# The two FFNs of a hybrid decoder layer: half of the tokens at a time, seven block products in place of eight

## The chip, the cores and the metric

The kernel runs on one core of a Trainium2 chip. The metric is the device time of one launch in microseconds (us), the median over several runs. The engines are named as the profile names them: PE is TensorE (PEld its weight loads), DVE is VectorE, ACT is ScalarE, POOL is GpSimd, SP is SyncE, which here only issues DMAs.

## The reference

One layer over 1032 tokens (1024 of a prompt, 8 of a decoding batch), all in float32. What the change touches are the two SwiGLU blocks, `ffn1` and `ffn2`, each with D_MODEL = 1024 and D_FF = 2816:

```python
def rmsnorm(x, g):
    y = xf * lax.rsqrt(jnp.mean(xf * xf, axis=-1, keepdims=True) + EPS)
    return y * g

def swiglu_half(x, g, w_gate, w_up, w_down):
    u = rmsnorm(x, g)
    return x + 0.5 * ((jax.nn.silu(u @ w_gate) * (u @ w_up)) @ w_down)

def hybrid_layer(...):
    h = swiglu_half(x, ffn1_norm, ffn1_w_gate, ffn1_w_up, ffn1_w_down)
    u = rmsnorm(h, mix_norm); z = u @ w_in          # latent attention, retention, gates
    ...
    h = h + merged @ w_out
    h = swiglu_half(h, ffn2_norm, ffn2_w_gate, ffn2_w_up, ffn2_w_down)
    gate = sigmoid(rmsnorm(h, ple_norm) @ w_ple_gate)
    h = h + gate * (p_emb @ w_ple_proj)             # then a last rmsnorm
```

## The kernel before

**Layout.** Activations stand transposed: features on the 128 partitions (8 tiles `h[0..7]` of 128 features), tokens along the free axis. The 1032 tokens are worked in three chunks of 344 (`CHUNKS`).

**Products.** A float32 product is made of three passes of split numbers: `split` (L92 to L94) casts a tile to a rounded high part on ACT (L93) and takes the rest, source minus high part, on DVE (L94); `mm3` (L127 to L130) then issues high x high, high x low, low x high, each a matmul with its own weight load, summed in PSUM. Weights come from DRAM by `Ring.load` (L103) in blocks of 128 x 1024 and are split once each.

**The norm.** `norm_steps` (L183) multiplies h by the gain, splits it into the two halves of `u` (ACT L199, DVE L200), squares it (ACT L144, L148) and adds the squares on POOL (L149). `rstd` (L162) sums over partitions with small matmuls (L169), iterates on DVE (`newton`, L133 to L137) and spreads the result back with matmuls (L177). The factor r itself is multiplied into the gate and up products after PSUM (L235, L238).

**An FFN** (`ffn`, L221) goes over the 22 tiles of D_FF in groups of three (the last of four). For each tile f it loads a gate and an up block, and for each chunk makes both products over 8 tiles of features (48 matmuls of 344 columns), then silu and the multiplication, and splits the result into `mid`. After a group come its down products into PSUM, over the group's tiles, added to h in SBUF (L274). One FFN so has 22 x 3 x 48 + 22 x 8 x 3 x 3 = 4752 matmuls of 344 columns. Nothing but the weights is moved: h and u stay in SBUF.

**At the seams** the work is interleaved by hand: the last group's down products hand each finished tile of h to the next norm (`nxt`, called step by step between products), the start of the first FFN splits u tile by tile while products run, and the last chunk group of `wout` does the same for the second FFN's norm (L980 and following). `pend`, `tick` and `flush` hold back the steps that wait for other engines. Behind the first FFN stand the value products of retention (`value_tile`, L321 to L323: 24 matmuls of 256 columns for each tile of 128 tokens), which need u alone; in front of the second FFN stands `wout`, behind it the per-layer embedding (`ple_gate`, L1034 and following).

The order on each engine is made from the program by a scheduler, within what the tiles' buffers allow; each engine runs its own list in that order.

## Time and profile before

| | |
|---|---|
| time, three runs | 2558.05, 2555.63, 2557.17 us; median 2557.17 us |
| span of the profiled execution | 2553.2 us, from its first to its last instruction, 4.0 us under the median of the runs |
| PE busy | 2519.5 us (99%), 16,612 matmuls |
| PEld busy | 2433.6 us (95%) |
| DVE busy | 1251.2 us (49%) |
| ACT busy | 655.8 us (26%) |
| POOL busy | 209.6 us (8%) |
| HBM traffic | 147.47 MB read, 19.94 MB written, 66 GB/s over the span |

A row of the timeline gives the start in us from the span's begin, the duration, engine, source line, operation, output and inputs, shape, count, and in brackets how long the engine had been idle and what ended that. A row of the windows view gives a stretch, then the busy time and count of instructions of PE, PEld, DVE, ACT and POOL, the granted TensorE clock, the share of the DMA engines and GB/s. A row of a line's instructions gives min/median/max in ns and the first and last start. Matmul durations overlap, since they are pipelined: the step from start to start is what one costs.

### The profile page before, as it was taken

Reading aid. Unit: us, or ns where it says so; the run is one execution under the profiler, and the core shown is the slowest. Engines: PE = TensorE matmul, PEld = TensorE weight load, DVE = VectorE, ACT = ScalarE, POOL = GpSimd, SP = SyncE. Lnnn points to the kernel's source line nnn. Section 1 sums busy time; section 2 is a strip of 40 time slices with the busy share of each in tenths; the row PEclk is TensorE's granted clock in tenths of the full one; section 3 lists DMA queues with packets and bytes.
Section 4 is the critical chain, followed back from the end, with each engine's and each line's share of the span. In section 5 each row is a group of like instructions: output and inputs, shape, how many; then the busy total and the mean of one; then the engine's idle time right before and its main releaser. Section 6 shows DMA issues by size and latency. Waiting matters only on the chain.

```text
span 2553.2 us, 40552 instructions
## 1 busy us (share of the span) xinstructions
PE 2519.5 (99%) x16612; PEld 2433.6 (95%) x16612; DVE 1251.2 (49%) x2744; ACT 655.8 (26%) x1302; POOL 209.6 (8%) x247
## 2 busy tenths in 40 slices
PE   8999999999999999999999999999999999999998
PEld 7999999999999999999996669999999999999997
DVE  6434334434354666522467776844434343343645
ACT  5121121211233111211145652431211211212521
POOL 3000000000022001100042100200000000000211
PEclk9999999999999999999999999999999999999999
DMA  4111111110113121221124436111111110111111
GB/s 151 42 59 51 41 59 42 50 42 34 58 71 117 62 77 58 98 77 64 54 78 129 121 107 217 51 58 42 50 42 44 53 53 34 58 42 50 40 36 67
DMA packets 82507, 171.08 MB, mean 67 GB/s; under 512 B 9401, under 2 KB 51586, under 8 KB 82322
## 3 DMA queue, kind: packets, MB, share of 16 engines
q1 hardware_dynamic: 76098, 150.67, 17.6%
q0 software_dynamic: 6224, 17.82, 2.0%
q8 instruction: 130, 2.13, 0.3%
q14 instruction: 55, 0.45, 0.1%
HBM read 147.47 MB, written 19.94 MB: 66 GB/s over the span
## 4 chain that ended last, share of the span: by engine, by line
PE 94%; DVE 3%; DMA 1%; ACT 1%; issue 1%; POOL 0%; SPq 0%; POOLq 0%; DVEq 0%; ACTq 0%
PE ps L128 27%; PE ps L129 27%; PE ps L130 27%; PE ps L732 2%; PE ps L768 1%; PE ps L757 1%; PE ps L177 1%; PE ps L323 1%; PE ps L321 1%; PE ps L322 1%; DVE u L200 1%; PE ps L169 1%; DMA raw<-in_wout_dram 0%; PE ps L906 0%; PE ps L880 0%
## 5 line engine op out<-in xcount | busy, mean ns | idle before, releaser
L128 PE MATMUL ps<-u,w 128*128 128x344 f32 (+2 forms) x3072 | 990.6, 323 | 7.6 <-ACT w L93 7.6
L129 PE MATMUL ps<-u,w 128*128 128x344 f32 (+2 forms) x3072 | 987.0, 321 | 3.5 <-DVE u L200 3.5
L130 PE MATMUL ps<-u,w 128*128 128x344 f32 (+2 forms) x3072 | 982.8, 320 | 0.1
L128 PEld LDWEIGHTS ps<-u,w 128*128 128x128 f32 x3072 | 578.4, 188 | 9.6 <-ACT w L93 7.6
L129 PEld LDWEIGHTS ps<-u,w 128*128 128x128 f32 x3072 | 577.2, 188 | 6.4 <-DVE u L200 5.5
L130 PEld LDWEIGHTS ps<-u,w 128*128 128x128 f32 x3072 | 577.9, 188 | 1.1 <-DVE w L94 0.5
L93 ACT CAST w<-raw 128x1024 fp32r<-128x1024 f32 (+1 forms) x198 | 203.4, 1042 | 776.7 <-PE ps L130 757.0
L130 PE MATMUL ps<-mid,w 128*128 128x344 f32 x1248 | 399.7, 320 | 0.1
L129 PE MATMUL ps<-mid,w 128*128 128x344 f32 x1248 | 399.7, 320 | 0.0
L128 PE MATMUL ps<-mid,w 128*128 128x344 f32 x1248 | 399.6, 320 | 0.0
L274 DVE SCALAR_TENSOR_TENSOR h<-ps,h 128x344 f32<-128x344 f32 x336 | 172.0, 515 | 242.0 <-PE ps L130 239.8
L94 DVE TENSOR_TENSOR w<-raw,w 128x1024 fp32r<-128x1024 f32 (+1 forms) x198 | 239.1, 1219 | 63.5 <-ACT w L93 63.0
L130 PEld LDWEIGHTS ps<-mid,w 128*128 128x128 f32 x1248 | 235.4, 189 | 0.4 <-DVE w L94 0.4
L128 PEld LDWEIGHTS ps<-mid,w 128*128 128x128 f32 x1248 | 235.2, 188 | 0.0
L129 PEld LDWEIGHTS ps<-mid,w 128*128 128x128 f32 x1248 | 235.0, 188 | 0.0
L238 DVE TENSOR_TENSOR m<-ps,r 128x344 f32<-128x344 f32 x132 | 68.1, 516 | 336.4 <-PE ps L130 336.4
L149 POOL TENSOR_TENSOR acc<-acc,sq 128x344 f32<-128x344 f32 x83 | 84.1, 1013 | 1677.9 <-ACT sq L148 1676.6
L93 ACT CAST mid<-m 128x344 fp32r<-128x344 f32 x156 | 74.9, 480 | 353.3 <-DVE m L239 316.6
L235 DVE TENSOR_TENSOR sg<-ps,r 128x344 f32<-128x344 f32 x132 | 68.0, 515 | 167.5 <-PE ps L130 166.0
L236 ACT ACTIVATE sg<-sg 128x344 f32<-128x344 f32 x132 | 64.6, 489 | 227.8 <-DVE sg L235 227.8
L94 DVE TENSOR_TENSOR mid<-m,mid 128x344 fp32r<-128x344 f32 x156 | 80.9, 519 | 48.0 <-ACT mid L93 46.9
L200 DVE SCALAR_TENSOR_TENSOR u<-h,gains,u 128x344 fp32r<-128x344 f32 x96 | 65.1, 686 | 30.7 <-ACT u L199 30.6
(247 smaller groups left out, 2321.4 us busy)
## 6 DMA issues: line engine op xcount, KB each, us to landing
ct<-in_cache_dram SPq DMA_DIRECT2D x128, 128.0 KB, 2.1
raw<-in_f1gate_dram SPq DMA_DIRECT2D x22, 512.0 KB, 3.5
raw<-in_f1up_dram SPq DMA_DIRECT2D x22, 512.0 KB, 3.5
raw<-in_f1down_dram SPq DMA_DIRECT2D x22, 512.0 KB, 4.5
raw<-in_f2gate_dram SPq DMA_DIRECT2D x22, 512.0 KB, 3.5
raw<-in_f2up_dram SPq DMA_DIRECT2D x22, 512.0 KB, 3.5
raw<-in_f2down_dram SPq DMA_DIRECT2D x22, 512.0 KB, 4.8
hs_d<-h POOLq DMA_DIRECT2D x3, 1376.0 KB, 6.1
```

The source lines that it names most:

```text
L93: act.copy(dst_hi, src)
L94: dve.tensor_tensor(dst_lo, src, dst_hi.bitcast(F32), op=ALU.subtract)
L128: pe.matmul(ps, w[:, 0, ws], x[:, 0, xs], start=start, stop=False)
L129: pe.matmul(ps, w[:, 0, ws], x[:, 1, xs], start=False, stop=False)
L130: pe.matmul(ps, w[:, 1, ws], x[:, 0, xs], start=False, stop=stop)
L149: pool.tensor_tensor(acc, acc, sq[:, :n], op=ALU.add)
L200: dve.scalar_tensor_tensor(u[k][:, 1, xs], h[k][:, xs], gain(gi, k), u[k][:, 0, xs].bitcast(F32), op0=ALU.mult, op1=ALU.subtract)
L235: dve.tensor_tensor(s[:, :n], pg[:, :n], r[:, xs], op=ALU.mult)
L236: act.activation(s[:, :n], s[:, :n], AF.Silu)
L238: dve.tensor_tensor(m[:, :n], pu[:, :n], r[:, xs], op=ALU.mult)
L274: dve.scalar_tensor_tensor(hv, ps[:, :n], 0.5, hv, op0=ALU.mult, op1=ALU.add)
L732: pe.matmul(ps[:, :w], qc[hd][:, i * P:(i + 1) * P], kc[hd][:, j:j + w], start=True, stop=not diag)
```

## The change

Both FFNs are rewritten; the rest of the layer is moved only where it joined onto them.

**Halves and blocks.** A half of the tokens (`tp`, 516 tokens) is worked at a time, as two column blocks of 258 (`HC`). Every product is cut into 2 x 2 blocks (features by halves, outputs by two tiles, tokens by the two column blocks) and made of seven block products (`ORDER`) of sums and differences, which are collected in PSUM and, for three of them, in copies: `unit` makes the two sets of seven for a pair of outputs, gate and up (`pair`) or two pairs of output tiles (`down`). A pair unit has 168 matmuls of 258 columns, a down unit 42 for each pair of D_FF tiles in its group. `GROUPS` has 3, 3, 2, 2 and 1 pairs. One FFN so has 5544 matmuls of 258 columns.

**Weights.** `Stream` loads eight raw blocks for a unit (2 outputs x 4 blocks, 128 x 512 for gate and up), makes four sums or differences of each four blocks on POOL (L267, L269, L287, L292) and splits fourteen blocks (ACT L102, DVE L103), five ahead of the product. This is done again for the second half of the tokens.

**Gated values.** The products of gate and up come out as four blocks. They are added, silu and multiplication made, three more sums made (L406 to L421, POOL), and seven blocks split into `mid`, which stays in SBUF.

**Inputs.** The seven block sums of the normed input (`b`) for the first half are made at the start from h (`first`); those of the second half are made during the first half's products (`second`), written to DRAM (L570), and read back in one go (L607) when the first half's last pair unit is done. r is now multiplied in before the products.

**Seams.** h goes to DRAM after each FFN (L477) and is read from there (L584, L632); the norms that were interleaved with products stand by themselves.

The core of the diff; of the two `evac`, the first is a pair unit's and the second a down unit's:

```diff
+HC = T // 4
+GROUPS = [(0, 1, 2), (3, 4, 5), (6, 7), (8, 9), (10,)]
...
+    ORDER = (0, 1, 2, 3, 4, 6, 5)
...
+        def early(self, r):
+            for s in range(2):
+                n = r["a11", s].shape[-1]
+                r["s1", s] = self.rawp.tile([P, 512], F32, tag="q", name="ws")[:, :n]
+                pool.tensor_tensor(r["s1", s], r["a21", s], r["a22", s], op=ALU.add)
+            for s in range(2):
+                pool.tensor_tensor(r["a21", s], r["a11", s], r["a21", s], op=ALU.subtract)
...
+        def make(self, units):
+            r = self.load(units[0])
+            self.early(r)
+            for i in range(len(units)):
+                nxt = None
+                for q, part in zip(ORDER, ("a11", "s1", "a11", "a12", "a21", "a12", "a22")):
+                    for s in range(2):
+                        yield self.split(r[part, s])
+                    if q == 0:
+                        for s in range(2):
+                            pool.tensor_tensor(r["a11", s], r["s1", s], r["a11", s], op=ALU.subtract)
+                    elif q == 2 and i + 1 < len(units):
+                        nxt = self.load(units[i + 1])
+                    elif q == 3:
+                        for s in range(2):
+                            pool.tensor_tensor(r["a12", s], r["a12", s], r["a11", s], op=ALU.subtract)
+                    elif q == 4 and nxt:
+                        self.early(nxt)
+                r = nxt
...
+    def unit(stream, b, kh, evac, tick, ahead=None):
+        x, y, z = ([take(), take()] for take in (xbank, ybank, zbank))
+        for q in ORDER:
+            if ahead is not None:
+                next(ahead, None)
+            for s in range(2):
+                w = stream.take()
+                ps = (x, z, x, y, x, x, z)[q][s][:, :HC]
+                for j in range(kh):
+                    js = slice(j * P, (j + 1) * P)
+                    t = b(q, j)
+                    pe.matmul(ps, w[:, 0, js], t[:, 0], start=q in (0, 1, 3) and j == 0, stop=False,
+                              skip_group_check=True)
+                    pe.matmul(ps, w[:, 0, js], t[:, 1], start=False, stop=False, skip_group_check=True)
+                    pe.matmul(ps, w[:, 1, js], t[:, 0], start=False, stop=j == kh - 1, skip_group_check=True)
+                evac(q, s, ps)
+                tick(at)
...
+            def evac(q, s, ps):
+                if q < 3:
+                    t = kept[s, q] = et()
+                    act.copy(t, ps)
+                    return
+                if q == 5:
+                    t = et()
+                    if s == 0:
+                        act.activation(t, ps, AF.Silu)
+                    else:
+                        dve.tensor_tensor(t, ps, gated[q], op=ALU.mult)
+                else:
+                    t = kept[s, {3: 0, 4: 1, 6: 2}[q]]
+                    dve.tensor_tensor(t, t, ps, op=ALU.add)
+                    if s == 0:
+                        defer(1, act.activation, t, t, AF.Silu)
+                    else:
+                        eng = dve if q == 6 else pool
+                        defer(2, eng.tensor_tensor, t, t, gated[q], op=ALU.mult)
...
+                def evac(q, s, ps):
+                    if q in (0, 2):
+                        t = et()
+                        act.activation(t, ps, AF.Copy, scale=0.5)
+                        defer(1, pool.tensor_tensor, hv, hv, t, op=ALU.add)
+                    else:
+                        dve.scalar_tensor_tensor(hv, ps, 0.5, hv, op0=ALU.mult, op1=ALU.add)
+                    if last and q == 5:
+                        sp.dma_start(dst[:, k - 1:k + 1, both(tp)], ht[:, k - 1:k + 1])
...
+                    if tp == 0 and seen == NF // 2:
+                        while side[0] is not None:
+                            tick(99)
+                        bt = new_b()
+                        for q in ORDER:
+                            sp.dma_start(bt[:, :, q].bitcast(F32), b_d[:, :, q])
...
+    ffn("f1", 0, a["xT"], hs_d, b1_d)
...
+        read_h(ht, hs_d)
+        wv0 = [ring.load("rv", i) for i in range(2)]
+        for c in range(NCH):
+            for _ in norm_steps(tmp, h, c, 1, u, r):
+                pass
...
-        u, r, wv0 = ffn(ring, tmp, mp, "f1", h, u, r, up, ws, lambda c: norm_steps(tmp, h, c, 0, u, r, c == 0),
-                        lambda: [ring.load("rv", i) for i in range(2)], to_mix)
...
+            wout(g, c, wo)
+            c0, n = CHUNKS[c]
+            sp.dma_start(h2_d[:, :, c0:c0 + n], ht[:, :, c0:c0 + n])
...
+    ffn("f2", 2, h2_d, h3_d, b2_d)
...
+    read_h(ht, h3_d)
```

**How the order moves: POOL in the FFN.** Before, the whole stretch of the first FFN on POOL holds the additions of squares for the norms at its two ends (`acc`, `sq`) and the writes of h for later; between them nothing:

```order
L149 ISA
L149 TENSOR_TENSOR acc<-acc,sq 128x344 x26
L331 DMA hs_d<-h 1024x1x344
L149 TENSOR_TENSOR acc<-acc,sq 128x344 x7
L331 DMA hs_d<-h 1024x1x344
```

Now one pair unit in the middle of an FFN half has these (`wq` a raw weight block, `ws` a sum, `e` a block of gated values):

```order
L380 TENSOR_TENSOR e<-e 128x258
L287 TENSOR_TENSOR wq<-ws,wq 128x512
L380 TENSOR_TENSOR e<-e 128x258
L287 TENSOR_TENSOR wq<-ws,wq 128x512
L406 TENSOR_TENSOR e<-e 128x258
L411 TENSOR_TENSOR e<-e 128x258
L416 TENSOR_TENSOR e<-e 128x258
L292 TENSOR_TENSOR wq<-wq 128x512
L267 TENSOR_TENSOR ws<-wq 128x384
L269 TENSOR_TENSOR wq<-wq 128x384
L421 TENSOR_TENSOR e<-e 128x258
```

POOL had no instruction between the two norms; it now has fourteen for each pair unit (a second L292, L267 and L269 follow), each with two inputs in SBUF.

**DVE in the FFN.** Before, one D_FF tile and one chunk on DVE (`sg`, `m` the gate and up values, `mid` the split result, `w` the split weights, two blocks for three chunks):

```order
L235 TENSOR_TENSOR sg<-ps_1453,r 128x344
L94 TENSOR_TENSOR w<-raw,w 128x1024
L238 TENSOR_TENSOR m<-ps_1454,r 128x344
L239 TENSOR_TENSOR m<-m,sg 128x344
L94 TENSOR_TENSOR w<-raw,w 128x1024
L94 TENSOR_TENSOR mid<-m,mid 128x344
```

Now a part of a pair unit:

```order
L103 TENSOR_TENSOR w<-wq,w 128x512
L434 TENSOR_TENSOR e<-ps_5925,e 128x258
L103 TENSOR_TENSOR w<-wq,w 128x512
L103 TENSOR_TENSOR mid<-e,mid 128x258
L103 TENSOR_TENSOR w<-wq,w 128x512
L103 TENSOR_TENSOR mid<-e,mid 128x258 x2
L103 TENSOR_TENSOR w<-wq,w 128x512
L103 TENSOR_TENSOR mid<-e,mid 128x258
L103 TENSOR_TENSOR w<-wq,w 128x512
L103 TENSOR_TENSOR mid<-e,mid 128x258
L103 TENSOR_TENSOR w<-wq,w 128x512 x3
```

The splits of weights, which read two tiles of SBUF each, now make up most of the list, fourteen to a pair unit.

**DVE at the end of the first FFN.** Before, the additions to h and the splits of the next norm's u alternate:

```order
L274 SCALAR_TENSOR_TENSOR h<-ps_6125,h 128x344
L200 SCALAR_TENSOR_TENSOR u_6106<-h,gains,u_6106 128x344
L274 SCALAR_TENSOR_TENSOR h<-ps_6143,h 128x344
L200 SCALAR_TENSOR_TENSOR u_6107<-h,gains,u_6107 128x344
L274 SCALAR_TENSOR_TENSOR h<-ps_6162,h 128x344
```

Now all of u comes behind the FFN's last addition:

```order
L475 SCALAR_TENSOR_TENSOR h<-ps_10629,h 128x258
L475 SCALAR_TENSOR_TENSOR h<-ps_10624,h 128x258
L475 SCALAR_TENSOR_TENSOR h<-ps_10625,h 128x258
L103 TENSOR_TENSOR w<-raw,w 128x1024 x3
L209 SCALAR_TENSOR_TENSOR u_10741<-h,gains,u_10741 128x344
L209 SCALAR_TENSOR_TENSOR u_10742<-h,gains,u_10742 128x344
```

The norm has moved from beside the last down products to behind them, and the value products, which read u, with it.

385 lines of the change are left out of this document (285 added, 100 removed).

## The prediction

> **What bounds the kernel now.** The page first: PE is busy over the whole span, DVE half of it, POOL hardly at all, and the chain that ended last runs over PE.
>
> ```profile
> span 2553.2 us, 40552 instructions
> PE 2519.5 (99%) x16612; PEld 2433.6 (95%) x16612; DVE 1251.2 (49%) x2744; ACT 655.8 (26%) x1302; POOL 209.6 (8%) x247
> PE 94%; DVE 3%; DMA 1%; ACT 1%; issue 1%; POOL 0%; SPq 0%; POOLq 0%; DVEq 0%; ACTq 0%
> ```
>
> So the stage of the change is set by what a matmul costs from start to start. The windows view of two stretches within the first FFN gives that for 344 columns, and the timeline gives the first and the last of a run of 24 value products for 256 columns.
>
> ```profile
> 200.00:400.00 200.00, 200.00 (x1269) 200.00 (x1268) 78.56 (x132) 34.35 (x53) 0.00 (x0) 1.00 0.13 44
> 400.00:700.00 300.00, 300.00 (x1902) 300.00 (x1901) 120.39 (x204) 50.69 (x78) 0.00 (x0) 1.00 0.14 47
> 778.81 0.28 PE L321 MATMUL ps<-w,u 128*128 128x256 f32 x1
> 781.54 0.28 PE L323 MATMUL ps<-w,u 128*128 128x256 f32 x1
> ```
>
> 300/1902 is 0.1577 us; (781.54 - 778.81)/23 is 0.1187 us, so 258 columns take 0.1187 x 258/256 = 0.1196 us. The price goes with the columns; a narrower matmul loses nothing by itself. POOL stands at zero in both windows: that is what the change ends.
>
> The same view over the whole stages shows what before loses in them:
>
> ```profile
> 7.60:778.80 771.20, 766.06 (x4818) 762.61 (x4819) 340.58 (x600) 175.98 (x296) 41.71 (x41) 1.00 0.16 56
> 1622.80:1665.50 42.70, 38.99 (x242) 38.07 (x241) 34.58 (x72) 23.86 (x50) 18.96 (x19) 0.96 0.04 14
> 1665.50:2418.50 753.00, 753.00 (x4796) 752.86 (x4795) 315.40 (x555) 154.45 (x251) 19.21 (x20) 1.00 0.13 46
> ```
>
> The first row is the first FFN, the third the second, each 4752 x 0.1577 = 749.4 us of products; the second row is the end of `wout`, 216 products (34.1 us) with the norm between them.
>
> **PE's part.** The two FFNs go from 9504 matmuls of 344 to 11,088 of 258: 1499 us to 1326 us, 173 us off, if PE stays the bound.
>
> **DVE and POOL.** These rows say that it won't. First the prices alone, from the views of single lines (min/median/max) and the groups by form:
>
> ```profile
> L149 POOL TENSOR_TENSOR acc<-acc,sq x83: 912/932/1782, 7.1 to 2419.4; 128x344 f32<-128x344 f32 x83
> L444 POOL TENSOR_TENSOR qd<-qT,qdec x8: 1281/1292/2293, 817.7 to 1023.4; 128x512 f32<-128x512 f32 x8
> L94 DVE TENSOR_TENSOR w<-raw,w x198: 678/1224/1946, 7.6 to 2478.9; 128x1024 fp32r<-128x1024 f32 x195, 128x512 fp32r<-128x512 f32 x3
> L94 DVE TENSOR_TENSOR mid<-m,mid x156: 502/516/1237, 28.5 to 2385.7; 128x344 fp32r<-128x344 f32 x156
> L238 DVE TENSOR_TENSOR m<-ps,r 128x344 f32<-128x344 f32 x132 | 68.1, 516 | 336.4 <-PE ps L130 336.4
> L93 ACT CAST w<-raw 128x1024 fp32r<-128x1024 f32 x195 | 201.7, 1049 | 772.1 <-PE ps L130 752.4 <-DMA raw<-in_batt_dram 12.9 <-DMA raw<-in_wout_dram 3.3
> L93 ACT CAST mid<-m 128x344 fp32r<-128x344 f32 x156 | 74.9, 480 | 353.3 <-DVE m L239 316.6 <-DVE m L967 30.0 <-PE ps L130 1.7
> ```
>
> POOL: (1292 - 932)/168 = 2.14 ns a column over a fixed 0.20 us. DVE: (1224 - 516)/680 = 1.04 ns a column over a fixed 0.16 us. ACT: (1049 - 480)/680 = 0.84 ns over 0.19 us. A pair unit (168 matmuls, 20.1 us of PE) has on ACT 14 casts of 512 (0.62 us), 6 copies, 4 silus and 7 casts of 258 (0.41 us each): 15.6 us, under PE. DVE has 14 of 512 (0.69 us) and 15 of 258 (0.43 us): 16.1 us. POOL has 8 of 512 (1.29 us) and 6 of 258 (0.75 us): 14.8 us. Each by itself fits under 20.1 us.
>
> But the maxima in those rows, twice the median, are no noise. The timeline at the start of before, where POOL adds squares while DVE splits, and a later moment where POOL rests:
>
> ```profile
> 11.75 6.89 POOL L149 TENSOR_TENSOR acc<-acc,sq 128x344 f32<-128x344 f32 x5 [0.33 <-ACT sq L148]
> 12.49 3.50 DVE L200 SCALAR_TENSOR_TENSOR u<-h,gains,u 128x344 fp32r<-128x344 f32 x3
> 43.34 1.55 DVE L200 SCALAR_TENSOR_TENSOR u<-h,gains,u 128x344 fp32r<-128x344 f32 x3
> ```
>
> Three L200, each with two inputs in SBUF, take 1.55 us alone and 3.50 us beside POOL, while POOL's five take 6.89 us for 4.66 us: they alternate, one pair in 3.50/3 = 1.17 us. Streaming alone is 344 x (2.14 + 1.04) = 1.09 us, so the streams do not overlap at all; only the fixed parts hide, but for 0.07 us a pair. L238, which reads PSUM and one SBUF tile, has no such spread: mean 516 ns.
>
> By this, what counts is the columns of POOL and of the two-input DVE instructions together. From the lists of the changed program, both FFNs: POOL 1132 instructions, 392,112 columns (352 x 512, 456 x 258, 128 x 384, 128 x 256, 64 x 128, 4 x 1032): 839 us, and 1132 x 0.07 = 79 us. DVE with two SBUF inputs 623,760 columns (616 x 512, 224 x 384, 224 x 256, 112 x 128, 528 x 258, 14 x 1032): 649 us. Sum 1567 us, less 12 us that lies ahead of the first products: **1555 us, more than PE's 1326 and more than the 1499 of before**. For one pair unit: 13.1 + 9.6 = 22.7 us against 20.1 us.
>
> How well the two fill this common time no row shows. Perfect filling is one end, 1555 us. Against it: a pair unit has 22 two-input instructions on DVE for 14 on POOL, so eight pay their fixed 0.16 us with nothing behind it, 1.3 us of 22.7; and both wait in order for PE, ACT and each other. I take 95%: 1555/0.95 = 1637 us; the other end is 90%, 1728 us. Against 1499 us of before the FFNs get **138 us longer** (56 to 229).
>
> The Trainium skill (page "SBUF — State Buffer", section "Who interferes with whom") says that a DVE instruction with two SBUF inputs contends with POOL's reads, and that the loser blocks for the whole instruction. The trace agrees on who contends; but held for whole instructions a pair would take 0.93 + 0.52 = 1.45 us, where the rows give 1.17 us. By the page's letter the sum is a rival below.
>
> **The seams.** Their prices come from the chain at the start of before, one row of the windows, and two groups:
>
> ```profile
> 2.20 6.14 DMA h<-in_xT_dram
> 18.69 0.83 PE ps L169 x6
> 23.69 0.45 ACT L180 COPY r<-ps 128x344 f32<-128x344 f32 x1 [4.88 <-PE ps L177]
> 10.00:20.00 10.00, 8.63 (x45) 7.50 (x44) 7.66 (x10) 7.17 (x13) 7.57 (x6) 1.00 1.02 371
> L199 ACT ACTIVATE u<-h,gains 128x344 fp32r<-128x344 f32 x96 | 55.1, 579 | 63.5 <-DVE h L274 42.7 <-DVE h L980 15.8 <-DMA h<-in_xT_dram 4.4
> ```
>
> Transfers run at 371 GB/s at best, a first one lands after about 6 us, and `rstd` takes 24.1 - 18.7 = 5.4 us. Start of the first FFN: 2.1 MB of h by 10 us, the last squares by 12, rstd to 17.4, four normed tiles (2 us) and a cast of 1032 (1.1 us): first product at 21 to 22 us where before had 7.6, **+14**. End of the first FFN: h back from DRAM (5 us), then three chunks of eight L200 and up to eight additions on POOL, 8 x 1.17 = 9.3 us or less each, and rstd: 37 us, in which PE can make about five value tiles (24 x 0.1187 = 2.85 us each) before its four PSUM banks wait for r: **+23**. Start of the second FFN, the first one's without the launch: **+19**. Its end: the same 37 us, with about 10 us of embedding products that need u alone: **+27**. The read-back of b, 7.4 MB at 371 GB/s, 20 us and 4 us of latency, stands on SP ahead of the last down weights and is covered by two down units of 10 us: **+8** for two; its cover gone it costs 24 us each. Sum +91. The writes of h wait on SP for the last additions, with weights of the next half behind them; those are wanted a down unit later, so that wait is hidden. What goes: the stalls within before's first FFN (771.2 - 749.4 = 21.8 us), its second (3.6 us) and the slowed end of `wout` (42.7 - 34.1 = 8.6 us): **-34**. Weights are read twice, about 70 MB an FFN in 800 us, some 86 GB/s of the 371: nothing.
>
> Sum: 2553.2 + 138 + 91 - 34 = 2748 us of span. The runs' median lies 4 us above before's span: **2752, say 2750 us**.
>
> **Rivals.** *PE stays the bound* (faster): if POOL and DVE overlap better than 12.49 to 15.99 us shows, FFNs take 1326 us, 24 us for two first units that DVE fills (16 us of normed splits on top of its 16.1), 19 us for eight units of one pair (5 us of PE, 7.4 of DVE): 1369 us, 130 us under before, so 2553 - 130 + 91 - 34 + 4 = 2484 us. For it: each engine alone fits. Against it: the 1.17 us. It decides at 1499 - 57 = 1442 us, where the seams are paid: the common time would have to shrink by 7% of its 1555. Chance 0.11.
>
> *The clock falls* (slower still):
>
> ```profile
> 32.00:36.00 4.00, 1.66 (x8) 0.92 (x6) 4.00 (x5) 3.23 (x9) 3.24 (x4) 1.00 0.01 4
> 36.00:40.00 4.00, 3.90 (x15) 3.90 (x16) 3.45 (x8) 3.65 (x9) 3.37 (x4) 0.52 0.00 0
> 40.00:44.00 4.00, 4.00 (x19) 4.00 (x18) 3.85 (x11) 0.76 (x2) 1.98 (x2) 0.63 0.00 0
> ```
>
> After 4 us with eight matmuls the granted clock is halved for about 7 us, worth 3 us. If starved products did that once in each of 44 pair units: 44 x 3 = 132 us more, about 2880 us. For it, PE will wait; against it, a unit's waits are some 0.3 us a product, far from a stretch of 4 us. Chance 0.05. The Trainium skill ("TensorE: Matmul & The Clock Gate", section "HAM oscillation — how this bites in real kernels") puts the limit at an idle gap of over about 3.4 us. The rows agree on the fall, but with PE busy for 1.66 of the 4 us.
>
> *Whole instructions exclude each other* (the page's letter): POOL 839 + 1132 x 0.20, DVE 649 + 1718 x 0.16, less 12: 1977 us for the FFNs, 478 us over before, 3092 us. The pairs of 1.17 us speak against it: 0.02.
>
> *Nothing gained, nothing lost*: filling so good and seams so short that the terms cancel: 0.02. That seven products do not replace eight is no rival: the program's list has 11,088 matmuls of 258.
>
> **How the numbers follow.** The common-time forecast has 0.80. About 0.2% (5 us) is what a measurement of this kernel can tell from no change. Faster 0.11; the same 0.02; slower 0.87. The likeliest case runs from 2640 us (perfect filling, shorter seams) to 2860 us (90%, longer ones); with better filling than my floor and with the clock's case the range is 2610 to 2890 us.
>
> **What would show it.** In the changed profile: POOL and two-input DVE instructions (L103, L267 to L292) at up to twice their times above, L475 and L437 at theirs; PE's busy count in a window of pair units 168 per 23 to 25 us, not per 20; PE waiting for DVE or ACT `w`; four holes in PE of about 20 us at the seams. Wrong: L103 of 512 columns at 0.69 us with POOL busy beside it, pair units of 20 us, or holes over 40 us.

## The result, and the profile after

The changed kernel takes 2912.84 us (median of 3 runs, 2912.58 to 2912.84) against 2557.17 us: a ratio of 1.139 with a 95% interval of 1.137 to 1.141. It is slower, as forecast, but 163 us above the 2750 us and 23 us above the upper end of the range. Where a kernel ran more than once, here and below, its time is the median of the runs that agree within 0.3%; one run of e13, of 5944.5 us, is left out of that.

The page of the changed kernel, to be read against the three lines at the head of the prediction:

```profile
span 2911.1 us, 51632 instructions
PE 2541.3 (87%) x18208; PEld 2384.7 (82%) x18208; DVE 2248.6 (77%) x4107; ACT 1243.5 (43%) x3029; POOL 1420.3 (49%) x1336
DVE 7%; PE 6%; issue 5%; POOL 3%; ACT 1%; DMA 1%; DVEq 0%; POOLq 0%; SPq 0%; ACTq 0%
```

PE fell from 99% to 87% busy, DVE rose from 49% to 77% and POOL from 8% to 49%; in what the page follows of the chain that ended last, a quarter of the span, DVE stands ahead of PE, which had 94%. The windows view of the changed kernel shows where (length; then busy time and count of PE, PEld, DVE, ACT, POOL; granted clock; DMA share; GB/s). The rows are the first FFN, the stretch from its last product to the last value tile, the stretch between `wout` and the second FFN, and the second FFN:

```profile
27.68:916.97 889.29, 755.84 (x5568) 722.51 (x5568) 797.17 (x1200) 441.99 (x1092) 617.11 (x560) 0.94 0.33 104
916.97:979.28 62.31, 41.81 (x269) 38.65 (x268) 36.15 (x69) 31.99 (x73) 26.68 (x27) 0.75 0.46 158
1835.32:1859.56 24.24, 5.73 (x28) 5.31 (x26) 11.90 (x40) 10.20 (x29) 0.00 (x0) 0.57 0.63 201
1859.56:2744.14 884.58, 749.94 (x5568) 717.32 (x5568) 793.02 (x1192) 437.58 (x1082) 617.91 (x560) 0.95 0.33 102
```

The FFNs take 889.3 + 884.6 = 1773.9 us; in the kernel before, 771.2 + 753.0 = 1524.2. That is 249.7 us more. DVE is busy for 1590 of the 1774 us. What lies outside of the FFNs grew from 2553.2 - 1524.2 = 1029.0 to 2911.1 - 1773.9 = 1137.2 us: 108.2 us more. Together 357.9 us, the difference of the two spans.

The forecast had 138 + 8 - 25.4 = 120.6 us for the FFNs (contention, the read-back of b, and the stalls within before's FFNs of 21.8 and 3.6 us) and 14 + 23 + 19 + 27 - 8.6 = 74.4 us for the seams. So 129 us of the miss are inside the FFNs and 34 us are at the seams.

The groups by form on DVE, the largest of them (mean ns of one behind the busy time):

```profile
L103 DVE TENSOR_TENSOR w<-wq,w 128x512 fp32r<-128x512 f32 x528 | 554.8, 1066 | 32.8 <-ACT w L102 27.5 <-PE ps L323 1.8
L103 DVE TENSOR_TENSOR mid<-e,mid 128x258 fp32r<-128x258 f32 x308 | 285.1, 937 | 80.0 <-ACT mid L102 80.0
L475 DVE SCALAR_TENSOR_TENSOR h<-ps,h 128x258 f32<-128x258 f32 x400 | 163.6, 413 | 5.9 <-PE ps L323 3.7 <-POOL wq L287 1.9
L437 DVE TENSOR_TENSOR e<-e,ps 128x258 f32<-128x258 f32 x264 | 108.6, 412 | 0.0
```

The instructions with two inputs in SBUF are stretched (1066 ns for a lone 0.69 us, 937 for a lone 0.42); those with one input in PSUM, of the same 258 columns, are not (413 and 412 ns). The contention is there, on the instructions that the prediction named. A pair unit, read off the start times of its 168 products, takes 21 to 26 us in the second halves (28 and 29 us for the first of each), 24.5 on average, as expected. Not expected were the down units: in the same halves 17.7 to 21.1 us for three blocks (15.1 of PE) and 14.0 to 17.5 us for most of those of two (10.0 of PE).

Two pair units of the same place in the program (`up6`), one in each FFN, bear on the rival of the clock without a run:

```profile
686.26:711.34 25.08, 22.68 (x171) 21.94 (x169) 22.18 (x30) 13.27 (x33) 17.22 (x16) 0.93 0.23 64
2514.74:2539.82 25.08, 21.37 (x171) 20.44 (x169) 22.17 (x30) 13.26 (x33) 17.23 (x16) 1.00 0.22 64
```

The granted clock was 0.93 in one and 1.00 in the other, and both take 25.08 us. The clock does fall, to 0.94 and 0.95 over the FFNs, but in this pair it falls inside time in which PE waits, and costs nothing. That it costs nothing in every unit is not shown.

### The profile page after: what moved, and what is told of

It reads as the page before. It is cut to its first block, busy times and chain, and to the rows that moved or that the text cites. A ratio compares the mean times of both kernels' runs of the same rounds, so it can differ in the third digit from the quotient of the medians.

```text
span 2911.1 us, 51632 instructions
## 1 busy us (share of the span) xinstructions
PE 2541.3 (87%) x18208; PEld 2384.7 (82%) x18208; DVE 2248.6 (77%) x4107; ACT 1243.5 (43%) x3029; POOL 1420.3 (49%) x1336
## 5 line engine op out<-in xcount | busy, mean ns | idle before, releaser
L103 DVE TENSOR_TENSOR w<-wq,w 128x512 fp32r<-128x512 f32 (+3 forms) x1008 | 893.1, 900 | 62.3 <-ACT w L102 52.6
L320 PE MATMUL ps<-b,w 128*128 128x258 f32 x2464 | 727.6, 296 | 133.4 <-ACT e L427 73.3
L323 PE MATMUL ps<-b,w 128*128 128x258 f32 x2464 | 718.2, 292 | 19.3 <-DVE w L103 19.3
L322 PE MATMUL ps<-b,w 128*128 128x258 f32 x2464 | 722.5, 293 | 6.8 <-DVE b L103 6.8
L320 PEld LDWEIGHTS ps<-b,w 128*128 128x128 f32 x2464 | 486.4, 198 | 155.9 <-ACT e L427 85.1
L102 ACT CAST w<-wq 128x512 fp32r<-128x512 f32 (+3 forms) x1008 | 506.0, 527 | 234.7 <-POOL wq L292 98.5
L323 PEld LDWEIGHTS ps<-b,w 128*128 128x128 f32 x2464 | 491.5, 200 | 28.3 <-DVE w L103 27.1
L322 PEld LDWEIGHTS ps<-b,w 128*128 128x128 f32 x2464 | 490.1, 199 | 8.6 <-DVE b L103 8.5
L320 PE MATMUL ps<-mid,w 128*128 128x258 f32 x1232 | 372.1, 303 | 69.3 <-DVE h L475 36.6
L323 PE MATMUL ps<-mid,w 128*128 128x258 f32 x1232 | 367.9, 301 | 35.9 <-DVE w L103 35.4
L322 PE MATMUL ps<-mid,w 128*128 128x258 f32 x1232 | 363.2, 296 | 0.0
L103 DVE TENSOR_TENSOR mid<-e,mid 128x258 fp32r<-128x258 f32 x308 | 285.1, 937 | 80.0 <-ACT mid L102 80.0
L138 PE MATMUL ps<-u,w 128*128 128x344 f32 (+4 forms) x960 | 310.6, 324 | 4.5 <-DVE u L209 4.5
L137 PE MATMUL ps<-u,w 128*128 128x344 f32 (+4 forms) x960 | 312.9, 326 | 0.0
L139 PE MATMUL ps<-u,w 128*128 128x344 f32 (+4 forms) x960 | 309.1, 322 | 0.0
L267 POOL TENSOR_TENSOR ws<-wq 128x512 f32<-128x512 f32 (+3 forms) x168 | 200.5, 1193 | 198.6 <-DMA wq<-in_f2gate_dram 174.3
L292 POOL TENSOR_TENSOR wq<-wq 128x512 f32<-128x512 f32 (+3 forms) x168 | 215.7, 1286 | 103.3 <-issue 58.4
L102 ACT CAST mid<-e 128x258 fp32r<-128x258 f32 x308 | 122.4, 409 | 319.5 <-POOL e L380 141.8
L287 POOL TENSOR_TENSOR wq<-ws,wq 128x512 f32<-128x512 f32 (+3 forms) x168 | 183.3, 1093 | 125.5 <-DVE w L103 121.6
```

What stands on the lines that cost most here:

```text
L102: act.copy(dst_hi, src)
L103: dve.tensor_tensor(dst_lo, src, dst_hi.bitcast(F32), op=ALU.subtract)
L137: pe.matmul(ps, w[:, 0, ws], x[:, 0, xs], start=start, stop=False)
L138: pe.matmul(ps, w[:, 0, ws], x[:, 1, xs], start=False, stop=False)
L139: pe.matmul(ps, w[:, 1, ws], x[:, 0, xs], start=False, stop=stop)
L267: pool.tensor_tensor(r["s1", s], r["a21", s], r["a22", s], op=ALU.add)
```

## The experiments

The theories as the runs were planned: (A) DVE is the limit, by its own work and a part of POOL's; (B) the prediction's common time, in which POOL and DVE's two-input instructions take turns, sets the time (it is called port time from here on; the traces show the turns, not a port); (C) weights come late, through the chain of POOL sum, ACT cast and DVE split with five products of lead; later (D), the order of work in ACT's and POOL's queues. Each time is one run, except where a ratio is given; the kernel before took 2554.0 to 2554.6 us beside them. "FFNs" is the time from first to last product of each FFN in the profiled execution, both added, and "rest" is the span without it. What is left out in e1 to e5, e7, e8, e12 and e14 changes the layer's results; the other kernels still compute the layer.

| kernel | us | FFNs | rest |
|---|---|---|---|
| before | 2557.2 | 1524 | 1029 |
| changed | 2912.8 | 1774 | 1137 |
| without weight sums (e1) | 2540.0 | 1409 | 1129 |
| sums of zeros, free to move (e2) | 2982.3 | first half of the first FFN 788, all others as e1 | |
| without the weights' low part (e3) | 2595.0 | 1460 | 1133 |
| ACT copies for DVE's additions to h (e4) | 2855.5 | 1724 | 1130 |
| sums made, not used (e5) | 2951.6 | 1808 | 1142 |
| pair chain on DVE (e6) | 2839.9 | 1707 | 1131 |
| one b (e7) | 2831.5 | 1700 | 1130 |
| one b, longer lead (e8) | 2830.4 | 1696 | 1133 |
| pair chain and h on DVE (e9) | 2818.7 | 1688 | 1133 |
| weight sums on DVE (e10) | 2684.0 | 1556 | 1126 |
| all on DVE (e11) | 2654.4 | 1525 | 1128 |
| POOL copies for sums (e12) | 2596.4 | 1468 | 1126 |
| all on DVE, regrouped (e13) | 2600.0 | 1466 | 1130 |
| all on DVE, one b (e14) | 2581.0 | 1452 | 1126 |
| half of the sums on DVE (e15) | 2804.2 | 1672 | 1131 |

### e1: no weight sums

```diff
         def early(self, r):
             for s in range(2):
-                n = r["a11", s].shape[-1]
-                r["s1", s] = self.rawp.tile([P, 512], F32, tag="q", name="ws")[:, :n]
-                pool.tensor_tensor(r["s1", s], r["a21", s], r["a22", s], op=ALU.add)
...
+                r["s1", s] = r["a21", s]
...
-                            pool.tensor_tensor(r["a11", s], r["s1", s], r["a11", s], op=ALU.subtract)
+                            pass
...
-                            pool.tensor_tensor(r["a12", s], r["a12", s], r["a11", s], op=ALU.subtract)
+                            pass
```

> Leaves out the 672 weight sums on POOL (L267, L269, L287, L292): each product takes an unsummed block as its weight. Three theories, against 2912.8 us of the changed kernel. (A) DVE is the limit: its time is its own work plus POOL's instructions that its two-input ones wait for, one for one, and its PSUM-reading work comes on top. Without the sums a pair unit has on DVE 16.1 us plus six short waits, so PE is the bound again at 20.1: pair units of 20.5 to 21 us for 24 to 26, down units of three blocks 15 to 16 us for 17.7 to 21, of two 11 to 12 for 14 to 17; some 287 us off, 2570 to 2680 us, L103 on 512 columns near 0.69 us for 1.07. (B) Common port time as on record, filled to 95%: PE is the bound, 2540 to 2600 us. (C) Latency: a product's weights come late through the chain POOL sum, ACT cast, DVE split with five products of lead. The chain loses its first link: 2600 to 2750 us, but L103 would not be what fell.

Measured 2540.04 us. The units of the second halves, where no second b is prepared, are 20.18 us for a pair, 15.2 for three blocks, 10.1 to 11.4 for two: PE at 20.18/168 = 0.1201 us a matmul, the forecast cadence. DVE's group of 512 columns:

```profile
L103 DVE TENSOR_TENSOR w<-wq,w 128x512 fp32r<-128x512 f32 x616 | 478.4, 782 | 102.2 <-ACT w L102 88.3 <-DMA wq<-in_f2down_dram 2.7 <-DMA wq<-in_f1down_dram 2.2
```

0.78 us for 1.07: what is left over the lone 0.69 us goes with POOL's other work. The time is below the ranges of (A) and (C) and at the lower end of (B)'s. By itself it does not part contention from latency, since the sums are gone as work and as a link of the chain; the next runs do.

### e2: as many sums, on zeros, that nobody waits for

```diff
-                pool.tensor_tensor(r["s1", s], r["a21", s], r["a22", s], op=ALU.add)
+                r["s1", s] = r["a21", s]
+                pool.tensor_tensor(side_t[:, :n], side_t[:, :n], side_t[:, :n], op=ALU.add)
...
-                pool.tensor_tensor(r["a21", s], r["a11", s], r["a21", s], op=ALU.subtract)
+                pool.tensor_tensor(side_t[:, :n], side_t[:, :n], side_t[:, :n], op=ALU.subtract)
```

> As the kernel before this one in the list (each product takes an unsummed block), but POOL does as many additions of the same width at the same places in its order, on a tile of zeros that nobody waits for. (A) The contention is all there, the dependency is gone: 2820 to 2915 us, L103 on 512 columns still near 1.07 us, down units of two blocks still 14 to 17 us. (C) Latency: as without the sums, 2600 to 2750 us.

Measured 2982.25 us, over both. The test went wrong: sums that wait for nothing don't stay at their places. In the built program they stand far ahead, so POOL ran nearly all of them in the first half of the first FFN:

```profile
74.00:829.80 755.80, 419.86 (x2692) 398.81 (x2691) 447.72 (x613) 219.00 (x548) 686.87 (x745) 0.76 0.21 67
829.80:1169.60 339.80, 336.34 (x2774) 334.17 (x2772) 282.33 (x563) 220.64 (x521) 95.07 (x106) 1.00 0.38 117
```

The first row is that half from 74 us on: POOL is busy for 687 of 756 us and pair units take 50 us, because the operations that PE does wait for stand behind the others in POOL's queue. The second row is the next half, with no sum left: 339.8 us, to the tenth what it takes without sums. So this run says what a full POOL queue does, not what was asked; e5 asks again.

### e3: the weights' low part left out

```diff
-            split(w[:, 0, :n], w[:, 1, :n], src)
+            act.copy(w[:, 0, :n], src)
...
-                    pe.matmul(ps, w[:, 1, js], t[:, 0], start=False, stop=j == kh - 1, skip_group_check=True)
+                    pe.matmul(ps, w[:, 0, js], t[:, 0], start=False, stop=j == kh - 1, skip_group_check=True)
```

> Leaves out the low part of the weights in the FFNs: the 1008 subtractions L103 on weights go, and the third matmul takes the high part again, so PE has as many matmuls. POOL's sums stay. (A) DVE keeps a third of its work, PE is the bound: pair units 20.1 to 21 us, down units of three blocks 15 to 16, of two 10 to 11.5; FFNs near 1400 us for 1773, so about 2540 us (2490 to 2620); POOL's 512 sums at their lone 1.29 us for 1.36 to 1.60. (C) Latency: the chain loses one of three links and POOL's sums and ACT's casts are as late as before: pair units over 22 us, 2700 us or more.

Measured 2594.95 us, within (A) and against (C). In the second halves, after the first unit, pair units take 20.2 to 20.7 us, those of three blocks 15.2, of two 10.1 to 10.9. POOL's sums of 512 columns, three groups of this kernel, against means of 1598, 1538 and 1357 ns for the same lines in the changed one:

```profile
L292 POOL TENSOR_TENSOR wq<-wq 128x512 f32<-128x512 f32 x88 | 121.2, 1378 | 125.8 <-ACT w L274 88.8 <-issue 32.9 <-DMA x<-in_xT_dram 1.9
L269 POOL TENSOR_TENSOR wq<-wq 128x512 f32<-128x512 f32 x88 | 116.9, 1329 | 4.3
L287 POOL TENSOR_TENSOR wq<-ws,wq 128x512 f32<-128x512 f32 x88 | 114.0, 1302 | 32.8 <-ACT w L274 32.5
```

In the second halves either side alone is hidden under PE: POOL's sums with little on DVE (here), DVE's splits with little on POOL (e1). Only both together are not.

### e4: DVE's additions to h left out

```diff
-                        dve.scalar_tensor_tensor(hv, ps, 0.5, hv, op0=ALU.mult, op1=ALU.add)
+                        act.activation(et(), ps, AF.Copy, scale=0.5)
```

> Leaves out the addition of the down products to h that DVE makes (L475, 400 instructions of 0.413 us): ACT copies these products out of PSUM to a spare tile instead, so banks are released as before. (A) DVE's PSUM-reading work is on the path, 4.1 us of each of the 40 down units: units of three blocks 15.5 to 17 us for 17.7 to 21, of two 11.5 to 13.5 for 14 to 17; 100 to 150 us off, about 2790 us (2760 to 2815). (B) The model on record, in which that work rides beside POOL's at no cost: 0 to 20 us off, 2893 to 2913 us.

Measured 2855.48 us: 57 us off, less than (A) and more than (B). The second unit of a group of three blocks falls to PE's 15.2 us (from 17.7), the first one stays at 20.6 (from 21.0). So DVE's reads of PSUM are not free, as the prediction had them. Whether they are wholly on the path this run can't say, since ACT took on 400 copies for them.

### e5: the sums are made and not used

```diff
+                r["t", s] = self.rawp.tile([P, 512], F32, tag="q", name="ws")[:, :n]
+                pool.tensor_tensor(r["t", s], r["a21", s], r["a22", s], op=ALU.add)
+                r["s1", s] = r["a21", s]
...
-                pool.tensor_tensor(r["a21", s], r["a11", s], r["a21", s], op=ALU.subtract)
+                pool.tensor_tensor(spare[:, :n], r["a11", s], r["a21", s], op=ALU.subtract)
...
+                            pool.tensor_tensor(spare[:, :n], r["t", s], r["a11", s], op=ALU.subtract)
```

> The 672 weight sums stay on POOL, beside the same instructions, and read the same blocks, but write tiles that nobody reads; each product takes an unsummed block. (A) Contention: DVE and POOL meet as before, 2830 to 2920 us, pair units 23 to 26 us, L103 on 512 columns 1.0 us or more. (C) Weights come late through the chain of sum, cast and split: the chain is as short as without the sums, 2530 to 2650 us, pair units of 20.2.

Measured 2951.62 us, 32 us above (A)'s range and 39 above the changed kernel. The weights no longer wait for POOL's results, and nothing was gained; L104 here is the line of the split:

```profile
L104 DVE TENSOR_TENSOR w<-wq,w 128x512 fp32r<-128x512 f32 x616 | 639.7, 1052 | 15.7 <-ACT w L103 7.6
```

The 512 columns take 1.05 us as before. (C) as priced falls: what costs the time is POOL's work beside DVE's, not the link of the sums in the chain. Loads still wait until POOL has read the tiles that they overwrite; e8, below, has more of these tiles.

### e6: the chain to the gated blocks on DVE

```diff
-                pool.tensor_tensor(blk["1"], blk[6], blk[3], op=ALU.subtract)
+                dve.tensor_tensor(blk["1"], blk[6], blk[3], op=ALU.subtract)
...
-                        eng = dve if q == 6 else pool
+                        eng = dve
```

> The six POOL operations of a pair unit that lead to the gated blocks (two multiplications L380, four subtractions L406 to L421; 264 in all) go to DVE. (A) DVE is the limit and waits for POOL one for one: DVE gets 6 x 0.43 = 2.6 us of its own and loses half of 6 x 0.62 us of waiting: pair units within 1 us of before, 2890 to 2960 us. (B) Common port time sets pair units: POOL 0.62 against DVE 0.27 us of it, 2.1 us less each, pair units near 22.3 us and 2800 to 2840 us. (D) Order: PE waits for ACT copies (L427) that stand behind a cast of a gated block, which waits for POOL's chain, which stands behind weight sums; without POOL in the chain those holes of 1.5 us go, two or so in each pair unit: 2770 to 2840 us, and the wait of ACT's L102 for POOL e, 263 us, is gone.

Measured 2839.88 us, 73 us off: (A) as priced is out, (B) and (D) both have it at their upper edge of 2840 us, and this run doesn't part them: DVE's chain also frees POOL. What (D) means is seen in the changed kernel's timeline of POOL and of ACT in a pair unit (start, length, what; in brackets the idle time before it):

```profile
779.90 1.42 POOL L292 TENSOR_TENSOR wq<-wq 128x512 f32<-128x512 f32 x1 [0.96 <-DVE w L103]
781.40 0.80 POOL L267 TENSOR_TENSOR ws<-wq 128x256 f32<-128x256 f32 x1
782.28 1.07 POOL L269 TENSOR_TENSOR wq<-wq 128x256 f32<-128x256 f32 x1
783.31 0.92 POOL L421 TENSOR_TENSOR e<-e 128x258 f32<-128x258 f32 x1
```

```profile
780.63 0.64 ACT L102 CAST w<-wq 128x512 fp32r<-128x512 f32 x1
784.26 0.41 ACT L102 CAST mid<-e 128x258 fp32r<-128x258 f32 x1 [2.99 <-POOL e L421]
784.57 0.37 ACT L427 COPY e<-ps 128x258 f32<-128x258 f32 x1
```

L421, the last step of the gated blocks, stands behind three weight sums. ACT has nothing to do but wait for it for 2.99 us, and the copy that frees PE's bank (L427) stands behind that wait. PE's longest waits in the changed kernel (in total, times, longest), and the group of PE with most of them in e6:

```profile
PE ps L320 <- ACT e L427: 73.3, 56, 4.2
PE ps L323 <- DVE w L103: 54.7, 72, 2.5
PE ps L320 <- DVE e L437: 42.0, 34, 2.3
```

```profile
L320 PE MATMUL ps<-b,w 128*128 128x258 f32 x2464 | 723.2, 294 | 94.5 <-DVE e L437 53.2 <-ACT e L427 24.9 <-ACT w L102 9.2
```

The prediction had PE wait for `w`: it does, for 54.7 us behind DVE and 21.0 us behind ACT, but the largest single group of its waits is the one for this copy. It falls from 73.3 to 24.9 us in e6, that for DVE's L437 rises from 42.0 to 53.2 us. The pair units of the second halves go from 24.5 to 23.0 us on average.

### e7 and e8: one b for both halves, then a longer lead

```diff
-                        side[:] = [second(), 0, 0.4, 0.0]
...
-                        bt = new_b()
-                        for q in ORDER:
-                            sp.dma_start(bt[:, :, q].bitcast(F32), b_d[:, :, q])
```

> Leaves out the preparation of the second half's b blocks and their read-back through DRAM: the second half multiplies by the first half's b. By the model on record it is worth 60 us of common port time, 63 at 95%, and 8 us of read-back: about 2842 us (2825 to 2855). From the changed kernel's own units, first against second half: 85 us, of which 13 belong to the first blocks: about 2840 us too. If it also keeps DMA or the clock busy in a way that slows units it doesn't stand in, more: under 2815 us.

Measured 2831.48 us: 81 us for the second half's b, within the range, beside the 71 us of the model on record and the 85 of the units, of which 13 belong to the first blocks. Then, on top of it:

```diff
-        wp = st.enter_context(pools(pre + "w", 6))
-        rawp = st.enter_context(pools(pre + "q", 16))
+        wp = st.enter_context(pools(pre + "w", 8))
+        rawp = st.enter_context(pools(pre + "q", 19))
...
-                        stream.ahead = 5
+                        stream.ahead = 7
```

> As the kernel before it (no second b), with the room put into a longer lead: products taken seven ahead for five, 8 split weight tiles for 6, 19 raw tiles for 16. (A, B) DVE and POOL are the limit on average: within 30 us of the kernel before it. (C) Weights are late only because the lead is short (five products are 3.6 us in a down unit of two blocks): 60 to 150 us under the kernel before it, down units of two blocks at 10 to 12 us for 14 to 17.

Measured 2830.44 us, 1 us less. A longer lead, with more tiles to load into, is worth nothing here; (C) falls a second time.

### e9: the additions to h on DVE as well

```diff
-                    if q in (0, 2):
-                        t = et()
-                        act.activation(t, ps, AF.Copy, scale=0.5)
-                        defer(1, pool.tensor_tensor, hv, hv, t, op=ALU.add)
-                    else:
-                        dve.scalar_tensor_tensor(hv, ps, 0.5, hv, op0=ALU.mult, op1=ALU.add)
+                    dve.scalar_tensor_tensor(hv, ps, 0.5, hv, op0=ALU.mult, op1=ALU.add)
```

> As the kernel with the six operations of a pair unit on DVE (2839.9 us), and the additions to h that POOL makes after a copy by ACT (L472, L380, 160 of them) are made by DVE straight from PSUM, as the other 400 are (0.413 us each). (A) DVE is the limit and waits out a bit more than half of POOL's time: 160 x 0.413 = 66 us more of its own against 0.55 x 160 x 0.62 = 55 us less waiting: 2835 to 2865 us. (B) Common port time at the filling of 0.87 to 0.89 seen so far: 160 x 0.62 = 99 us of it less, 60 to 110 us off, 2730 to 2780 us.

Measured 2818.66 us over three rounds (ratio to the kernel before 1.103, interval 1.101 to 1.105): 21 us off, between (A) and (B), nearer to (A).

### e10 and e11: the weight sums, then everything, on DVE

```diff
-                pool.tensor_tensor(r["s1", s], r["a21", s], r["a22", s], op=ALU.add)
+                dve.tensor_tensor(r["s1", s], r["a21", s], r["a22", s], op=ALU.add)
...
-                            pool.tensor_tensor(r["a12", s], r["a12", s], r["a11", s], op=ALU.subtract)
+                            dve.tensor_tensor(r["a12", s], r["a12", s], r["a11", s], op=ALU.subtract)
```

> The 672 weight sums go from POOL to DVE, all else as in the changed kernel. Common port time falls from 1537 us by 625 and rises by 281 to 1193 us, under PE's 1326; DVE's own work rises from 1193 by 388 to 1581 us. (A) DVE is the limit: 1581 us and 0.6 of POOL's remaining 283: 1750 us, 98% busy, 1790 us of FFNs for 1774: 2890 to 2960 us, pair units about 24 to 25 us, DVE over 95% busy. (B) Common port time: PE and DVE by turns set units, about 1650 us of FFNs, 2760 to 2820 us.

Measured 2684.01 us, 229 off: far below (A), below (B) as well.

> Weight sums, the six operations of a pair unit and all additions to h on DVE; POOL has almost nothing in the FFNs. Two-input instructions then take their lone times (512 columns 0.69 us). DVE's own work is 1193 + 388 + 114 + 66 = 1761 us, which no contention stretches: both theories say that it is the bound, 1761/0.98 = 1797 us of FFNs, 2900 to 2970 us; that is, contention with POOL costs about as much as doing POOL's work. If instead the order of work loses the 11%, units still fill badly: over 3000 us.

Measured 2654.36 us, 258 off, where both theories expected 2900 or more. The busiest of the engines got all of POOL's work, and the kernel is faster. The windows of its FFNs, and of the first one's second half:

```profile
24.21:786.87 762.66, 716.09 (x5568) 694.32 (x5568) 740.94 (x1743) 436.04 (x1010) 37.26 (x18) 0.97 0.38 120
1724.34:2486.18 761.84, 718.12 (x5568) 696.49 (x5568) 737.28 (x1734) 432.72 (x1002) 38.55 (x18) 0.97 0.38 119
430.20:786.87 356.67, 347.10 (x2773) 339.14 (x2772) 351.14 (x832) 208.63 (x480) 0.00 (x0) 0.99 0.34 107
```

DVE runs 1743 instructions in 741 us where it ran 1200 in 797; POOL is empty in the second half, and pair units there, after the first, take 20.2 us. L103 on 512 and on 258 columns is at its lone time:

```profile
L103 DVE TENSOR_TENSOR w<-wq,w 128x512 fp32r<-128x512 f32 x528 | 360.6, 691 | 13.6 <-ACT w L102 13.0
L103 DVE TENSOR_TENSOR mid<-e,mid 128x258 fp32r<-128x258 f32 x308 | 128.3, 418 | 3.4 <-ACT mid L102 3.2
```

What was wrong in (A) is the price of DVE's own work. The timeline of DVE here:

```profile
609.52 0.55 DVE L103 TENSOR_TENSOR w<-wq,w 128x384 fp32r<-128x384 f32 x1
609.99 0.41 DVE L470 SCALAR_TENSOR_TENSOR h<-ps,h 128x258 f32<-128x258 f32 x1
610.32 0.42 DVE L421 TENSOR_TENSOR e<-e 128x258 f32<-128x258 f32 x1
610.66 0.42 DVE L103 TENSOR_TENSOR mid<-e,mid 128x258 fp32r<-128x258 f32 x1
```

One starts before the record of the one ahead has ended: 384 columns cost 0.47 us of the queue, not 0.55, and 258 cost 0.33 or 0.34, not 0.42. The fixed part is about 0.07 us, not the 0.16 us that the prediction took from the lengths of records. At these prices DVE's queue in the FFNs is 1454 us for the 1761 expected, and they took 1525. The Trainium skill says so ("Perfetto Trace Analysis", section "Optimizing Scalar/DVE Operations"): the latency of a profiled instruction holds about twice its overhead, since the second half overlaps with the next instruction. The same section warns that moving work between DVE and GpSimd might not help, as they share a port; here moving it away from GpSimd helped by 258 us.

### e12: POOL copies in place of sums

```diff
-                pool.tensor_tensor(r["s1", s], r["a21", s], r["a22", s], op=ALU.add)
+                pool.tensor_copy(r["s1", s], r["a21", s])
...
-                            pool.tensor_tensor(r["a12", s], r["a12", s], r["a11", s], op=ALU.subtract)
+                            pool.tensor_copy(r["a12", s], r["a11", s])
```

> Each of the 672 weight sums is replaced by a POOL copy of one of its blocks to the same place (one input for two, the same dependencies); products take the copies. If only POOL instructions with two inputs keep DVE waiting, DVE's L103 on 512 columns takes 0.69 to 0.78 us and the time is that of the kernel without sums, 2530 to 2580 us. If any POOL instruction on SBUF does, L103 stays at 0.9 us or more, and the time falls only as far as a copy is shorter than a sum: 2700 to 2900 us.

Measured 2596.38 us, between the two. DVE's split and one of POOL's copies:

```profile
L103 DVE TENSOR_TENSOR w<-wq,w 128x512 fp32r<-128x512 f32 x528 | 451.0, 863 | 49.2 <-ACT w L102 43.2
```

```profile
L267 POOL COPY ws<-wq 128x512 f32<-128x512 f32 x88 | 68.6, 782 | 187.9 <-ACT w L102 167.7 <-DMA wq<-in_f1gate_dram 13.3 <-DMA wq<-in_f2gate_dram 2.5
```

A copy has one input and still holds DVE up (0.86 us; 0.78 without sums, 0.69 alone), but it is over in 0.68 to 0.90 us for a sum's 1.36 to 1.60. The chain of POOL, ACT and DVE has all its links here, and pair units of the second halves run at 20.2 us: a third sign against (C).

### e13, e14 and e15: what is left

With all on DVE, groups of 3, 3, 2 and 3 pairs, and b read back in pieces:

```diff
-GROUPS = [(0, 1, 2), (3, 4, 5), (6, 7), (8, 9), (10,)]
+GROUPS = ((0, 1, 2), (3, 4, 5), (6, 7), (8, 9, 10))
...
+                read_b(bt, 2 if o == 0 else 7)
...
-                        for q in ORDER:
-                            sp.dma_start(bt[:, :, q].bitcast(F32), b_d[:, :, q])
+                        late += ORDER
+                        read_b(bt, 2)
```

> As the kernel with all on DVE (2654.4 us), with eight down units in a half for ten (groups of 3, 3, 2 and 3 pairs), so DVE reads PSUM 28 times less in each half, 28 x 0.33 = 9 us, and with the second half's b read back two and then five blocks at a time instead of in one piece ahead of the last down weights. If DVE's whole queue is what sets the down units: 12 us less in each of four halves, and the hole of 10 us in each first half is gone: 2580 to 2620 us. If the down units there are set by something else (weights from DRAM, PE waiting for banks): over 2635 us.

Measured 2600.02 us, as expected; ratio to the kernel before 1.018 (interval 1.016 to 1.020). This is the fastest version found that still computes the layer, and it is slower than the kernel before: its FFNs are 58 us under before's 1524, the rest 101 us over before's 1029. All on DVE and one b (the edits of e11 and e7 together):

> As the kernel with all on DVE (2654.4 us), leaving out the second half's b and its read-back (the second half multiplies by the first half's b). First halves there take 406 us and second halves 356; 13 of the 50 belong to the first blocks. So 2 x 36 us off: 2565 to 2600 us. What then still lies over the kernel before, 10 to 45 us, is seams alone, since the FFNs are then about 1450 us for 1524.

Measured 2581.02 us, as expected: with the FFNs at 1452 us the seams alone, 97 us, keep it above before. And half of the sums on DVE, from the changed kernel:

```diff
-                pool.tensor_tensor(r["s1", s], r["a21", s], r["a22", s], op=ALU.add)
+                dve.tensor_tensor(r["s1", s], r["a21", s], r["a22", s], op=ALU.add)
...
-                pool.tensor_tensor(r["a21", s], r["a11", s], r["a21", s], op=ALU.subtract)
+                dve.tensor_tensor(r["a21", s], r["a11", s], r["a21", s], op=ALU.subtract)
```

> The changed kernel with the first four of each unit's eight weight sums (L267, L269; 336 of the 672) on DVE. Theory as revised: FFN time is DVE's whole queue at its start-to-start prices (0.61 us for 512 columns, 0.33 for 258 from PSUM) and about 0.8 of POOL's time at the port. POOL gives up 312 us of that, worth 250, DVE takes on 168: 82 us off, about 2830 us (2800 to 2850). Half of what moving all 672 brought would be 115 us, 2798. If the gain comes only once POOL is out of the weights' chain altogether: over 2860 us.

Measured 2804.19 us, within the range: 109 us off, 47% of what all of them bring, about in proportion to the work moved.

## Why the prediction was right in direction and wrong in size

**The cadence was right.** 0.1196 us was forecast for 258 columns; units that nothing holds up run at 0.1201. PE's part of the sum, 1326 us for both FFNs, is a floor that second halves without contention come near: 340 us in e1 for 332.

**The contention was right, and it is the cause of the longer FFNs.** In the second halves sums alone (e3) and splits alone (e1) lie under PE; together they don't, leaving the sums' results unused takes nothing off (e5), and with POOL's work on DVE the time goes, though DVE has more to do (e11). Who contends was right too: L475 and L437 with one input in PSUM kept their 0.41 us.

**The step that failed is the filling**: "How well the two fill this common time no row shows. [...] I take 95%: 1555/0.95 = 1637 us; the other end is 90%, 1728 us." The common time was right: by the same prices, the instructions that started within the FFNs of the changed kernel add up to 1537 us. But the FFNs took 1774: 87%, below the low end. The prediction let everything else on DVE lie under POOL's time at the port: its reads of PSUM (708 instructions, 189 us by columns) and its fixed parts (2390 instructions of 0.07 us, 167 us). With all of these 357 us hidden, the FFNs would take 1537 us; with none of them, 1894. Measured is 1774, so 237 us of 357 lay in the open, where the 5% left room for 82.

Put in another way, DVE's whole queue at its start-to-start prices, 633 us for the columns of two-input instructions with the 189 and 167, is 990 us, and of POOL's 904 us at the port DVE stood still for (1774 - 990)/904 = 0.87. The moves to DVE give this rate each by itself, as (what the FFNs gained + what DVE took on) / what POOL gave up. DVE takes on 1.04 ns a column and 0.07 us an instruction, POOL gives up 2.14 ns and 0.07 us; for all sums, 270,336 columns in 672 instructions, that is 328 and 626 us:

- half of the sums (e15): (102 + 164)/313 = 0.85
- all sums (e10): (218 + 328)/626 = 0.87
- the pair chain (e6): (67 + 89)/164 = 0.95
- the additions to h, after it (e9): (19 + 54)/100 = 0.73
- the sums, after both (e11): (163 + 328)/626 = 0.78

By this account a microsecond of POOL at the port costs DVE 0.7 to 0.95 us, and the same columns cost DVE itself only 1.04 of POOL's 2.14 ns: that is why all on DVE is faster. The rates of e10 and e11 are low if anything, since most pair units of their second halves already stand at PE's 20.2 us. The highest of the rates, e6, goes with the holes behind L421, so the order of the queues has a part there; how the 237 us divide between the order and the meeting of instructions was not separated. That DVE's reads of PSUM were really among them was tried: e4 takes 400 of them away, 132 us, and the FFNs gain 50, with ACT copying in their place.

One sum could have shown it beforehand, that of a down unit by itself: it has ten of these reads, 3.3 us, in 10 to 15 us of PE. By the same prices a unit of three blocks has 15.2 us of common time, and 19.6 us with its reads of PSUM and all fixed parts of DVE. Two in a row take 38.7 to 39.6 us in the second halves, so hardly anything of these was hidden. A pair unit has 22.7 us, and 26.6 with them, and takes 24.5: there about half was. (These are estimates; weights are made five products ahead, so the work of two units overlaps at the border.)

**The seams were undersized, all of them; this is the smaller part of the miss, 34 us.** Start of the first FFN: 27.68 us for 7.60, +20 where +14 was forecast. From the first FFN's end to the second's start: 942.6 us for 886.7, +56 where 23 + 19 - 8.6 = 33 was forecast; of it the second FFN's start is 24.2 us (19 forecast), in which h alone keeps ACT waiting 8.5 us on its way through DRAM, and the first value product comes 9.3 us after the last product (5 forecast). End: 166.9 us for 134.7, +32 for +27. Of the 6 us that the first start is over, POOL's sums have a good part: without sums on POOL the first product starts at 23.30 us (e1), with everything on DVE at 24.21 (e11).

**The read-back of b** was forecast at 8 us. The units of two blocks that were to cover it keep their time: the second takes 10.7 us in first halves and 11.3 and 10.8 in second ones. The next unit, of one block, whose weights are loaded behind b, does not. Here it is in the first FFN's first half and second half:

```profile
474.96:486.22 11.26, 7.88 (x44) 6.81 (x43) 7.10 (x22) 5.49 (x20) 7.96 (x16) 0.85 0.32 99
901.62:908.26 6.64, 5.98 (x44) 5.39 (x43) 6.36 (x20) 4.21 (x17) 5.55 (x10) 1.00 0.09 23
```

Without a second b (e7) it takes 6.7 us in first halves too. That is 4.6 us each; over the last four units of a first half, 46.5 us for e7's 43.8, 2.6 us each: 5 to 9 us for two, so the 8 was about right. The first unit of the second half takes 28 and 29 us for e7's 24 as well; how much of that is the read-back was not separated. The cover was real: with units shortened (e11) the second unit of two blocks takes 21.3 and 21.1 us for 11.5, and without the read-back (e14) 11.5 in first halves too.

**The rivals.** PE as the bound (FFNs of 1369 us) was wrong for this kernel; without the sums it is near (1409 us in e1). The clock fell, and in the one pair of units that could be compared it cost nothing. Whole instructions that exclude each other (3092 us) priced too high, though single ones do wait in that way, below.

## What to carry to other kernels

Before work is given to an idle POOL, ask whether DVE beside it runs instructions with two inputs in SBUF: then POOL's time is in part DVE's time, in this kernel 0.7 to 0.95 us for one, and POOL, at twice DVE's time a column, was the wrong place even though DVE was the busier engine. Price an engine's queue by start-to-start times, not by the lengths of single records, and price each kind of unit by itself: a sum over pair and down units hid that down units would miss. Where two limits share a resource, what lies beside it is hidden only in part; a filling that no row shows needs a wider range than the 90 to 100% given here; it was 87%.
